# A block of two layers on one core: ends of stages, first pairs and first loads rearranged

## The chip, the core and the metric

One core of a Trainium2 chip. Five engines with their own instruction queues work on it: TensorE (PE in the profile; its weight loads are PEld), VectorE (DVE), ScalarE (ACT), GpSimd (POOL) and SyncE (SP), which here only issues transfers; POOL issues some too. Each queue runs in order; semaphores order the engines among each other. The metric is the device time of one execution in microseconds (us), lower is better; the kernel before has three such runs.

## What is computed

One block of a diffusion backbone for 256 latent and 256 context tokens of width 2048, float32, in two layers. Each layer is a mixer and a squared-ReLU MLP (2048 to 8192 and back), each between two norms and with a shift, a scale and a gate that a large matrix (`ada_w`) makes from the conditioning vector `c`.

```
layer 0:  h  = mod(norm(x));  xx = shifted(h) - h
          k, v, r  = (h + xx*mu) @ w_k, w_v, w_r          one mu each
          decay, a = low ranks of width 96 (two directions);  gate = low rank of width 256
          per head (32 of 64) and direction, token by token:
              S = S*decay - (S kk) b^T + v k^T;   out = S r       kk = norm(k*k_k), b = kk*a
          y  = (groupnorm(out) + bonus) * gate @ w_o
layer 1:  z = conv3(h @ in_w);  v, x1, x2 = split(z)
          y = x2 * conv(h2, x1 * conv(h1, v))       long filters h1, h2 from a small sine network
          y = y @ out_w
each:     x += gate * norm(y);   then the same around  relu(h @ up)^2 @ down
```

## The kernel before, in words

All large products run as three products of two halves: a float32 operand is cast to fp32r on ACT (`wh`, `xh`), the rest is subtracted on DVE (`wl`, `xl`), and PE adds hi*hi, hi*lo and lo*hi in one PSUM bank. `load_split` loads a block of weights on SP and splits it; `gemm_ws` keeps two column blocks of 128 in two banks (`mm`) over the whole contraction, `gemm_tok` one column block of 512 for two halves of the tokens (`tt`). With `lead` the first call takes two such groups at once in four banks. In the listing nearly all instructions of ACT, DVE and SP have line 53, the wrapper that records them, and those of PE line 111, so groups are told apart by their tiles.

The stages, in order: `start` loads and normalizes, makes the first shift and scale, mixes the tokens for the low ranks (`mix_split` 1, 4, 5) and for the key (`mix_split` 2, kept in `self.xs`), and multiplies the low ranks into six banks. `lora_hidden` empties these banks through `xt`. `rwkv_proj` is the key projection (`mm<-xh,wh`); in each half pair `tick` takes units of a background: second halves of the low ranks (`lora2`, 44 of its 80 units), the mixes of value and receptance (`mixes`, 24 units, tile `xs`, stored to memory as `xv`, `xr`), and `ada_w` columns on DVE (`acc`, 70 units). `rwkv_begin` runs the first two fills (`fill_r`, `fill_v`: products of value and receptance for a group of four heads, tile `fl`) beside the rest of the low ranks and the first group's preparation. `rwkv_scan` runs the recurrence in eight groups of eight steps in chunks of 64 tokens (tiles `VU`, `NT`, `KR`, `Z`), with the next group's fills and preparation between; in the last group `filters` takes the place of the fills: three sine layers, then sixteen blocks, each a product with split weights (`w4h`, `w4l`, tile `sg`) and a transform (`fl`). Then `rwkv_out`, the first MLP, `hyena`, the second MLP. Each of these four ends in `resid`: squares of the result's rows (`ysq`, `ss`), root, reciprocal, a diagonal matrix `dg`, and with it PE turns the result (`sg<-dg`), which is added to `x`.

The order of each queue comes from a planner: it simulates the program and picks for each engine the ready instruction that was traced first; `high_priority(n)` counts an instruction as traced n places earlier. Two things go ahead of it. `add_manual_dep` chains: while `self.pins` is a dict, every instruction of the engines in `self.pinned` is tied behind the one traced before it, so that these queues run in the order of the code. In `start` that is PE alone, in the loop of `rwkv_scan` (from `self.pins = {}` on) PE, ACT, DVE and SP. And a tile waits for the memory that an earlier pool used there: the scan's pools open when those of the projection close.

Of the kernel before, what the change touches and what calls it, by code (L numbers as in the profile page):

```python
# [18 lines left out]
P = 128  # L19
# [50 lines left out]
class Kern:  # L70
# [105 lines left out]
    def gemm_ws(self, W, K, ms, x, ntok, evac, lead=False):  # L176

        nk = K // P
        if lead:
            ps = [[self.mm.tile([P, 512], F32, name="mm") for _ in range(2)] for _ in range(2)]  # L180
            for k0 in range(0, nk, 4):
                w = [self.load_split(W[k0 * P : (k0 + 4) * P, m0 * P : (m0 + 2) * P].rearrange("(k p) n -> p k n", p=P), 4, 256)
                     for m0 in ms[:2]]
                for k in range(4):
                    for j in range(2):
                        for i in range(2):
                            self.mm3(ps[j][i][:, :ntok], self.cut(w[j][k], slice(i * P, (i + 1) * P)), x(k0 + k),
                                     k0 + k == 0, k0 + k == nk - 1)
                self.tick(self.rate)
            for j in range(2):  # L190
                for i in range(2):
                    evac(ms[j] + i, ps[j][i][:, :ntok])
            ms = ms[2:]
        for m0 in ms:
            ps = [self.mm.tile([P, 512], F32, name="mm") for _ in range(2)]
            for k0 in range(0, nk, 8):
                src = W[k0 * P : (k0 + 8) * P, m0 * P : (m0 + 2) * P].rearrange("(k p) n -> p k n", p=P)
                w = self.load_split(src, 8, 256)
                for k in range(8):
                    for i in range(2):  # L200
                        s = slice(i * P, (i + 1) * P)
                        self.mm3(ps[i][:, :ntok], self.cut(w[k], s), x(k0 + k),
                                 k0 + k == 0, k0 + k == nk - 1)
                self.tick(self.rate)
            for i in range(2):
                evac(m0 + i, ps[i][:, :ntok])

    def gemm_tok(self, W, x, evac, lead=False, stages=None):

        for ns in ((0, 1), (2,), (3,)) if lead else ((0,), (1,), (2,), (3,)):  # L210
            ps = {(n, tt): self.mm.tile([P, 512], F32, name="mm") for n in ns for tt in range(2)}
            for k0 in range(0, KT, 4):
                if stages and len(ns) > 1:
                    stages(k0)
                for n in ns:
                    w = self.load_split(W[k0 * P : (k0 + 4) * P, n * 512 : (n + 1) * 512].rearrange("(k p) n -> p k n", p=P), 4, 512)
                    for k in range(k0, k0 + 4):
                        for tt in range(2):
                            self.mm3(ps[n, tt], self.cut(x(k), slice(tt * P, (tt + 1) * P)), w[k - k0], k == 0, k == KT - 1)
# [122 lines left out]
    def ada_scan(self, n, pool):  # L342
# [4 lines left out]
        nc.vector.memset(wide, 0.0)  # L347
        nc.vector.tensor_copy(wide[:, :, 0], self.sc2[:, 0, :])
        pick = pool.tile([P, 2], F32, name="pick", bufs=1)
        nc.vector.memset(pick, 0.0)  # L350
        for j in range(4):
            nc.vector.tensor_tensor(pick, pick, self.ident[:, 32 * j : 32 * j + 2], op=ALU.add)
# [75 lines left out]
    def resid(self, x, y, ss, layer, gi, ch, pool, nxt=None):  # L428
# [12 lines left out]
        for n in range(1, 4):  # L441
            nc.vector.tensor_tensor(ss[:, 0, :], ss[:, 0, :], ss[:, n, :], op=ALU.add)
        nc.scalar.activation(ss[:, 1, :], ss[:, 0, :], AF.Sqrt, bias=self.eps[:, 0:1], scale=1.0 / D)
        nc.vector.reciprocal(ss[:, 1, :], ss[:, 1, :])
        dg = pool.tile([P, 2, P], F32, name="dg", bufs=1)
        for tt in range(2):
            nc.vector.tensor_scalar(dg[:, tt], self.ident, ss[:, 1, tt : tt + 1], None, op0=ALU.mult)
# [33 lines left out]
    def filters(self, es):  # L481
# [3 lines left out]
        p2 = self.pool(es, "f2", 2)  # L485
        fw = p1.tile([33, 64], F32, name="fw")
# [10 lines left out]
        for m, (lhs, n) in enumerate(((fw[:], 64), (w23[:], 64), (w3[:].rearrange("p a b -> p (a b)"), P))):  # L497
# [13 lines left out]
            if m == 2:  # L511
                self.tables()
            yield
# [9 lines left out]
        dft = []  # L523
        for i, nm in enumerate(("dftc", "dfts")):
            dft.append(self.dft_load(nm, p1, p2, "hf", 3))
        w4s = []

        def load(i):
            dc, o = divmod(i, 2)
            if dc < 4:  # L530
                w4 = p2.tile([P, 512], F32, name="w4")
                for b in range(2):
                    c0 = (b * 2 + o) * D + dc * 512
                    nc.sync.dma_start(w4[64 * b : 64 * b + 64, :], I["f_w4"][0, :, c0 : c0 + 512])
                w4s.append(w4)

        def skip(i):
            dc, o = divmod(i, 2)
            if dc < 4:
                self.sk = p2.tile([P, 512], F32, name="sk", bufs=1)[0:1, :]  # L540
                nc.sync.dma_start(self.sk, I["skip"][0, o : o + 1, dc * 512 : (dc + 1) * 512])

        def window(dc):
            if dc < 4:
                self.win = p2.tile([P, 2, 512], F32, name="win", bufs=1)
                nc.sync.dma_start(self.win, I["window"][:, dc * 512 : (dc + 1) * 512].rearrange("(a p) d -> p a d", p=P))

        window(0), load(0), skip(0)

        def first(dc, o, e, put):  # L550

            if not e:
                w4 = w4s.pop(0)
                self.w4 = split2(w4)
                load(2 * dc + o + 1)
            for tt in range(2):
# [4 lines left out]
                if o and e and tt:  # L561
                    window(dc + 1)
                if e == 0 and tt == 0:
# [6 lines left out]

        def split2(x):
            return self.split_into(p2.tile([P, 512], F32R, name="w4h")[:], x[:], p2.tile([P, 512], F32R, name="w4l")[:])
# [85 lines left out]
    def shifted(self, k):  # L658
# [3 lines left out]
        t = self.xt.tile([P, 512], F32, name="sx", bufs=2)  # L662
# [85 lines left out]
    def rwkv_proj(self, l2, ad1):  # L748
# [6 lines left out]
        self.bg, self.rate = [self.beside(mixed, self.NLOW + 24, ad, n)], (self.NLOW + 24 + n) / 15  # L755
# [17 lines left out]
        self.gemm_ws(I["w_k"][0], D, range(0, KT, 2), lambda k: xs[k], 512, evk)  # L773
# [179 lines left out]
    def rwkv_begin(self):  # L953
# [5 lines left out]
        for _ in self.beside(itertools.chain(self.fill_v(0), self.fill_r(1)), 48, self.low, n - n // 8 + .1):  # L959
            self.tick(self.BEG)  # L960
# [3 lines left out]
    def rwkv_scan(self, es, prep_pools, ngroups=KT // 2):  # L964
# [486 lines left out]
    def rwkv_out(self, xp):  # L1451
        nc, tc = self.nc, self.tc
        with tc.tile_pool(reuse_waits="tile", name="oy", bufs=16) as oy, tc.tile_pool(reuse_waits="tile", name="op", bufs=1) as op:
# [9 lines left out]

            def ev(n, tt, ps):
# [48 lines left out]
    PRT = 1  # L1513
# [4 lines left out]
    KEARLY = 16  # L1518
# [7 lines left out]
    SLACK = 0  # L1526
# [127 lines left out]
    def start(self, ap, xp):  # L1654
# [16 lines left out]
        self.pins, self.pinned = {}, ("pe",)  # L1671
# [5 lines left out]
        for q in range(4):  # L1677
# [4 lines left out]
            for k in range(4 * q, 4 * q + 4):  # L1682
# [5 lines left out]
                sx = self.shifted(k)  # L1688
                for n, m in enumerate((1, 4)):
# [8 lines left out]
        self.xs += [self.mix_split(2, k, True, self.xm) for k in range(self.KEARLY, KT)]  # L1698
# [171 lines left out]
```

## Time and profile before

| | us |
|---|---|
| three runs | 3592.66, 3605.2, 3619.01 (median 3605.2) |
| profiled execution | 3607.2 |
| its span in the trace | 3605.3 |
| `start` (to the key's first matmul) | 196.5 |
| key projection | 234.1 |
| `rwkv_begin` | 124.7 |
| scan, filters and last readout | 855.1 |
| `rwkv_out` to the first `dg` product | 101.3 |
| first MLP to its `dg` | 786.1 |
| `hyena` to its `dg` | 541.0 |
| second MLP to its `dg` | 750.5 |

The page tells the busy time of each engine; the stages above are cut from it at the first matmuls of each. PE means matmuls, PEld weight loads beside them. "Idle before" in a line is the time that the engine stood still before an instruction, with the work that ended it. PEclk is the clock that the chip granted PE, as a share of 2.4 GHz. SPq is SP's queue of transfers.

### The profile page before, as it was taken

What the parts mean: (1) busy time and instruction counts of PE and PEld (TensorE: products, weight loads), DVE (VectorE), ACT (ScalarE), POOL (GpSimd) and SP (SyncE); (2) the same over time, 40 slices, a digit from 0 to 9 for tenths busy, and PEclk for the clock granted to TensorE, in tenths of its full rate; (3) what the DMA queues carried; (4) which work ended last, traced back from release to release, by engine and by line L of the source; (5) the groups of instructions that cost most, each with busy time, mean ns of one, the idle gap of its engine ahead of it and who ended that gap; (6) DMA issues with size and microseconds to landing.
All of it is one profiled execution on the core that took longest, in us unless ns stands there. A gap on an engine that the chain in (4) does not pass through costs nothing.

```text
span 3605.3 us, 74531 instructions
## 1 busy us (share of the span) xinstructions
PE 3326.2 (92%) x30598; PEld 2904.8 (81%) x30598; DVE 2457.0 (68%) x3867; ACT 1739.7 (48%) x3069; POOL 435.0 (12%) x496
## 2 busy tenths in 40 slices
PE   6799978989989788999999999999999899999999
PEld 3477777878888666898978889899887798989897
DVE  4788675767767655687777776587787675555554
ACT  4454454544544444443434435566664663434343
POOL 0011121111111000000000002034441540000000
PEclk8999998999999989999999999999999999999999
DMA  9678798988988635688888887566665775555553
GB/s 305 229 232 266 252 329 252 282 267 262 288 269 267 194 124 184 198 269 280 257 286 259 283 268 233 164 221 219 222 209 182 244 249 191 183 187 187 187 185 120
DMA packets 587807, 836.79 MB, mean 232 GB/s; under 512 B 39551, under 2 KB 373280, under 8 KB 587464
## 3 DMA queue, kind: packets, MB, share of 16 engines
q1 hardware_dynamic: 556360, 718.76, 62.1%
q0 software_dynamic: 31104, 113.26, 10.0%
q8 instruction: 239, 3.92, 0.5%
q14 instruction: 104, 0.85, 0.1%
HBM read 777.31 MB, written 54.59 MB: 231 GB/s over the span
## 4 chain that ended last, share of the span: by engine, by line
PE 49%; DMA 21%; DVE 14%; ACT 6%; issue 6%; POOL 2%; SPq 1%; ACTq 0%; DVEq 0%; POOLq 0%
PE mm L111 34%; DMA aw<-in_ada_w 10%; PE fl L111 5%; PE sg L111 5%; PE sc L111 4%; DVE wl L53 3%; DMA w<-in_mlp_down 2%; DVE acc L53 2%; DMA w<-in_mlp_up 2%; POOL acc L325 2%; ACT wh L53 2%; DVE tmp L53 1%; ACT aw L53 1%; DVE d L53 1%; DMA a<-a 1%
## 5 line engine op out<-in xcount | busy, mean ns | idle before, releaser
L53 DVE TENSOR_TENSOR wl<-w,wh 128x1024 fp32r<-128x1024 f32 (+1 forms) x716 | 918.6, 1288 | 548.7 <-ACT wh L53 546.8
L53 ACT CAST wh<-w 128x1024 fp32r<-128x1024 f32 (+1 forms) x716 | 738.1, 1043 | 744.4 <-PE mm L111 436.2
L111 PE MATMUL mm<-hxh,wh 128*128 128x258 f32 x2816 | 803.5, 287 | 13.2 <-DVE nt L53 11.9
L111 PE MATMUL mm<-hxh,wl 128*128 128x258 f32 x2816 | 801.5, 285 | 6.8 <-DVE wl L53 6.7
L111 PE MATMUL mm<-hxl,wh 128*128 128x258 f32 x2816 | 799.4, 284 | 0.0
L111 PEld LDWEIGHTS mm<-hxh,wh 128*128 128x128 f32 x2816 | 534.2, 190 | 17.0 <-DVE nt L53 13.8
L111 PEld LDWEIGHTS mm<-hxh,wl 128*128 128x128 f32 x2816 | 534.1, 190 | 10.7 <-DVE wl L53 9.3
L111 PEld LDWEIGHTS mm<-hxl,wh 128*128 128x128 f32 x2816 | 536.3, 190 | 1.8
L325 POOL TENSOR_TENSOR acc<-acc,aw 128x512 f32<-128x512 f32 x180 | 274.9, 1528 | 1360.2 <-ACT aw L53 1254.1
L111 PE MATMUL mm<-wh,uh 128*128 128x512 f32 x1024 | 405.4, 396 | 1.0 <-DVE nt L53 1.0
L111 PE MATMUL mm<-wl,uh 128*128 128x512 f32 x1024 | 400.5, 391 | 4.2 <-DVE wl L53 4.1
L111 PE MATMUL mm<-wh,ul 128*128 128x512 f32 x1024 | 402.3, 393 | 0.0
L53 DVE SCALAR_TENSOR_TENSOR acc<-aw,sc,acc 128x512 f32<-128x512 f32 x300 | 225.3, 751 | 89.6 <-DMA aw<-in_ada_w 87.0
L111 PEld LDWEIGHTS mm<-wl,uh 128*128 128x128 f32 x1024 | 192.3, 188 | 51.1 <-DVE wl L53 8.3
L111 PEld LDWEIGHTS mm<-wh,ul 128*128 128x128 f32 x1024 | 192.1, 188 | 45.6
L111 PEld LDWEIGHTS mm<-wh,uh 128*128 128x128 f32 x1024 | 192.3, 188 | 42.5 <-DVE nt L53 1.4
L111 PE MATMUL fl<-fh,fx 128*128 128x256 f32 x1024 | 213.1, 296 | 9.9 <-DMA fx<-xv 8.4
L53 ACT ACTIVATE aw<-aw,sc 128x512 f32<-128x512 f32 x180 | 125.8, 719 | 138.1 <-DMA aw<-in_ada_w 137.6
L111 PEld LDWEIGHTS fl<-fh,fx 128*128 128x128 f32 x1024 | 168.2, 193 | 27.9 <-issue 14.0
L111 PE MATMUL fl<-flo,fx 128*128 128x256 f32 x512 | 146.0, 285 | 0.4 <-issue 0.4
L111 PE MATMUL sg<-ard,KB 64*64 64x64 f32 (+1 forms) x3584 | 131.1, 247 | 13.5 <-ACT yf L53 4.8
L111 PE MATMUL mm<-xl,wh 128*128 128x512 f32 (+1 forms) x320 | 131.7, 412 | 12.1 <-DVE xl L53 12.0
(352 smaller groups left out, 5871.8 us busy)
## 6 DMA issues: line engine op xcount, KB each, us to landing
aw<-in_ada_w SPq DMA_DIRECT2D x288, 512.0 KB, 5.7
w<-in_mlp_down SPq DMA_DIRECT2D x128, 1024.0 KB, 5.1
w<-in_mlp_up SPq DMA_DIRECT2D x120, 1024.0 KB, 6.0
fx<-xv POOLq DMA_DIRECT2D x128, 512.0 KB, 6.2
aw<-in_ada_w SPq DMA_DIRECT2D x192, 256.0 KB, 3.0
w<-in_hy_in_w SPq DMA_DIRECT2D x44, 1024.0 KB, 6.2
fx<-xr POOLq DMA_DIRECT2D x64, 512.0 KB, 5.6
w<-in_w_k SPq DMA_DIRECT2D x16, 1024.0 KB, 5.7
```

The lines of the kernel that those rows point to most:

```text
L53: return self.kern.pin(self.key, f(*a, **kw))
L111: return self.pin("pe", self.nc.tensor.matmul(out, lhsT=lhsT, rhs=rhs, **kw))
L325: nc.gpsimd.tensor_tensor(acc, acc, w[:, a], op=ALU.add)
```

## The change

- `gemm_ws` and `gemm_tok`: in the last block of the contraction, the matmuls of the first bank (or pair, or half of the tokens) all come before those of the second. `gemm_tok`'s last column block (`3 in ns`) is emptied with priority PRT, now 400; the norm of `resid` up to `dg` has it too. `rwkv_out` calls one root of a small tile (`st`) before its products.
- `gemm_ws(first=...)`: the key's first pair takes two banks of pool `sc` instead of `mm`, and does not tick the background; the rate goes from 1/15 to 1/13 of the units.
- `KEARLY` 12 instead of 16: the last four key mixes are traced behind the loop over the low ranks, with the shift tiles kept (`sx` in four buffers).
- `LOWS` = 1.25: the rest of the low ranks is dealt out earlier among the fills.
- The first two `scan_values` (loads of `VU`) are traced first in `rwkv_scan` with priority PRS = 1000; the `memset`s and additions for `wide` and `pick` in `ada_scan` have PRS too.
- `filters`: the first loads of window, weights and skip come first; the two transform matrices are loaded and split between the sine layers; the weights of a block are split at the end of the block before (`weights`), not at its own beginning.

```diff
-    def gemm_ws(self, W, K, ms, x, ntok, evac, lead=False):
+    def gemm_ws(self, W, K, ms, x, ntok, evac, lead=False, first=None):
...
-                for k in range(4):
-                    for j in range(2):
-                        for i in range(2):
-                            self.mm3(ps[j][i][:, :ntok], ...)
+                order = [(j, k) for k in range(4) for j in range(2)]
+                for j, k in sorted(order) if k0 == nk - 4 else order:
+                    for i in range(2):
+                        self.mm3(ps[j][i][:, :ntok], ...)
...
-            ps = [self.mm.tile([P, 512], F32, name="mm") for _ in range(2)]
+            ps = first or [self.mm.tile([P, 512], F32, name="mm") for _ in range(2)]
...
-                self.tick(self.rate)
+                if not first:
+                    self.tick(self.rate)
...
+            first = None
...
-                    for k in range(k0, k0 + 4):
-                        for tt in range(2):
-                            self.mm3(ps[n, tt], ...)
+                    pairs = [(k, tt) for k in range(k0, k0 + 4) for tt in range(2)]
+                    for k, tt in sorted(pairs, key=lambda p: p[1]) if k0 == KT - 4 else pairs:
+                        self.mm3(ps[n, tt], ...)
...
-            for n in ns:
-                for tt in range(2):
-                    evac(n, tt, ps[n, tt])
+            with self.tc.high_priority(self.PRT if 3 in ns else 0):
+                for n in ns:
+                    for tt in range(2):
+                        evac(n, tt, ps[n, tt])
...
+        with self.tc.high_priority(self.PRS):          # ada_scan: wide, pick
...
+        with self.tc.high_priority(self.PRT):          # resid: ss, root, reciprocal, dg
...
+        def weights(i):                                # filters
+            halves.append(split2(w4s.pop(0)))
+            load(i)
+        halves, dft = [], []
+        window(0), load(0), load(1), skip(0)
...
             if m == 2:
                 self.tables()
+            else:
+                nm = ("dftc", "dfts")[m]
+                dft.append(self.dft_load(nm, p1, p2, "hf", 3))
+            if m == 1:
+                weights(2)
             yield
...
-                w4 = w4s.pop(0)
-                self.w4 = split2(w4)
-                load(2 * dc + o + 1)
+                self.w4 = halves.pop(0)
...
+                if e and tt and w4s:
+                    weights(2 * dc + o + 3)
...
-        t = self.xt.tile([P, 512], F32, name="sx", bufs=2)
+        t = self.xt.tile([P, 512], F32, name="sx", bufs=4)
...
-        self.bg, self.rate = [self.beside(mixed, self.NLOW + 24, ad, n)], (self.NLOW + 24 + n) / 15
+        self.bg, self.rate = [self.beside(mixed, self.NLOW + 24, ad, n)], (self.NLOW + 24 + n) / 13
...
-        self.gemm_ws(I["w_k"][0], ..., 512, evk)
+        self.gemm_ws(I["w_k"][0], ..., 512, evk, first=[self.sc.tile([P, 512], F32, name="sc") for _ in range(2)])
...
-        for _ in self.beside(itertools.chain(self.fill_v(0), self.fill_r(1)), 48, self.low, n - n // 8 + .1):
+        for _ in self.beside(itertools.chain(self.fill_v(0), self.fill_r(1)), 48, self.low, self.LOWS * (n - n // 8)):
...
+        with self.tc.high_priority(self.PRS):
+            for i in range(2):
+                self.scan_values(0, i)
         for _ in self.scan_products(0, 0):
             pass
         self.load_to(3 + self.AHEAD)
         self.feed_open(ngroups)
-        for i in range(2):
-            self.scan_values(0, i)
...
+            nc.scalar.activation(op.tile([P, 2], F32, name="st"), self.eps, AF.Sqrt)
...
-    PRT = 1
+    PRT = 400
-    KEARLY = 16
+    KEARLY = 12
+    LOWS = 1.25
+    PRS = 1000
...
-        self.xs += [self.mix_split(2, k, True, self.xm) for k in range(self.KEARLY, KT)]
+        self.xs += [self.mix_split(2, k, True, self.xm, sxs[k]) for k in range(self.KEARLY, KT)]
```

## Rows read from the trace of the kernel before

**Rows 1.** The page, part 1: busy us, share of span, instructions.

```profile
PE 3326.2 (92%) x30598; PEld 2904.8 (81%) x30598; DVE 2457.0 (68%) x3867; ACT 1739.7 (48%) x3069; POOL 435.0 (12%) x496
```

**Rows 2.** Windows: length, busy us of PE/PEld/DVE/ACT/POOL (count), PEclk, DMA share, GB/s.

```profile
196.50:430.60 234.10, 225.50 (x960) 180.65 (x960) 183.49 (x285) 105.20 (x168) 35.84 (x49) 0.96 0.79 261
...
1276.30:1403.00 126.70, 114.27 (x1224) 85.68 (x1224) 67.83 (x120) 57.55 (x124) 0.00 (x0) 0.94 0.36 118
```

**Rows 3.** Windows behind three stops.

```profile
2838.69:2846.00 7.31, 7.16 (x34) 6.68 (x35) 4.06 (x9) 4.96 (x11) 2.98 (x3) 0.59 0.78 260
562.80:575.50 12.70, 8.25 (x108) 7.14 (x108) 5.71 (x15) 3.84 (x10) 0.50 (x1) 0.52 0.57 172
196.50:200.00 3.50, 3.50 (x9) 2.81 (x10) 3.50 (x5) 3.48 (x8) 0.00 (x0) 0.58 0.77 223
```

**Rows 4.** DVE groups, 157 to 196.5: count, busy us, mean ns, idle before.

```profile
L53 DVE TENSOR_TENSOR xl<-xt,xh 128x512 fp32r<-128x512 f32 (+1 forms) x20 | 11.9, 615 | 0.0
L53 DVE SCALAR_TENSOR_TENSOR xt<-sx,cols,hall 128x512 f32<-128x512 f32 (+1 forms) x17 | 11.3, 681 | 0.0
L53 DVE SCALAR_TENSOR_TENSOR acc<-aw,sc,acc 128x512 f32<-128x512 f32 x12 | 8.9, 744 | 0.6 <-DMA aw<-in_ada_w 0.6
```

**Rows 5.** Order of time, PE: start, length, [idle before, releaser].

```profile
193.17 0.28 PE L111 MATMUL sg<-xh,wl 128*128 128x256 f32 x1
196.50 0.79 PE L111 MATMUL mm<-xh,wh 128*128 128x512 f32 x1 [3.05 <-ACT xt L53]
```

**Rows 6.** Waits, ACT, 196.5 to 430.6: total us, times, longest.

```profile
ACT xs L53 <- DMA xv<-xs: 31.4, 13, 5.0
```

**Rows 7.** Order of time, SP's queue, 524 to 574.

```profile
525.11 1.03 SPq L53 DMA_DIRECT2D v<-fe  x2
...
551.30 0.32 SPq L53 DMA_DIRECT2D gate<-l2t  x1
...
556.47 0.41 SPq L53 DMA_DIRECT2D fr<-in_w_v  x1
556.93 9.27 SPq L53 DMA_DIRECT2D VU<-v  x12
566.31 1.07 SPq L53 DMA_DIRECT2D aw<-in_ada_w  x2
```

**Rows 8.** Order of time, PE, 546 to 592.

```profile
562.83 1.04 PE L111 MATMUL sc<-VU,NT 64*64 64x64 f32 x12 [7.49 <-DMA VU<-v]
...
570.76 1.08 PE L111 MATMUL mm<-aw,wide 128*32 128x256 f32 x8 [4.43 <-DVE pick L53]
```

**Rows 9.** Order of time, DVE, same stretch.

```profile
556.24 0.42 DVE L53 TENSOR_TENSOR NT<-sg,masks 128x256 f32<-128x256 f32 x1
```

**Rows 10.** Waits, PE, 1276.4 to 1403.

```profile
PE sg L111 <- ACT w4h L53: 14.4, 7, 6.0
PE sg L111 <- DVE w4l L53: 1.4, 6, 0.2
```

**Rows 11.** Order of time, PE, at the four ends of stages.

```profile
1511.65 1.65 PE L453 MATMUL sg<-dg,o 128*128 128x128 f32 x6 [5.33 <-DVE dg L53]
...
2297.72 1.28 PE L453 MATMUL sg<-dg,o 128*128 128x128 f32 x8 [3.56 <-DVE dg L53]
...
2838.69 2.81 PE L453 MATMUL sg<-dg,y 128*128 128x128 f32 x9 [9.99 <-DVE dg L53]
...
3589.16 2.07 PE L453 MATMUL sg<-dg,o 128*128 128x128 f32 x8 [2.70 <-DVE dg L53]
```

**Rows 12.** Order of time, ACT, at the first and third end.

```profile
1509.49 1.28 ACT L53 ACT_TABLE_LOAD   x1
1510.78 0.30 ACT L53 ACTIVATE ss<-ss,eps 128x2 f32<-128x2 f32 x1
...
2831.55 1.33 ACT L53 ACTIVATE aw<-aw,sc 128x512 f32<-128x512 f32 x2 [2.93 <-DMA aw<-in_ada_w]
```

**Rows 13.** Order of time, PE, first MLP's first stop.

```profile
1557.98 0.58 PE L111 MATMUL mm<-hxh,wh 128*128 128x258 f32 x1 [3.66 <-DVE nt L53]
```

More of the change, by code (lines that the diff above doesn't have):

```diff
@@ L346, in ada_scan @@
         wide = pool.tile([P, KT, 32], F32, name="wide", bufs=1)
-        nc.vector.memset(wide, 0.0)
-        nc.vector.tensor_copy(wide[:, :, 0], self.sc2[:, 0, :])
         pick = pool.tile([P, 2], F32, name="pick", bufs=1)
-        nc.vector.memset(pick, 0.0)
-        for j in range(4):
-            nc.vector.tensor_tensor(pick, pick, self.ident[:, 32 * j : 32 * j + 2], op=ALU.add)
+        with self.tc.high_priority(self.PRS):
+            nc.vector.memset(wide, 0.0)
+            nc.vector.tensor_copy(wide[:, :, 0], self.sc2[:, 0, :])
+            nc.vector.memset(pick, 0.0)
+            for j in range(4):
+                nc.vector.tensor_tensor(pick, pick, self.ident[:, 32 * j : 32 * j + 2], op=ALU.add)
         todo = [(layer, ch, i, half, k4) for layer, ch, i in itertools.islice(self.ada_todo, n) for half in range(2) for k4 in range(4)]
@@ L439, in resid @@
                 self.split_into(hi[:, :, c], self.mod[:, nxt[0], nxt[2], :], lo[:, :, c])
[L441 to L444, printed above, removed]
         dg = pool.tile([P, 2, P], F32, name="dg", bufs=1)
-        for tt in range(2):
-            nc.vector.tensor_scalar(dg[:, tt], self.ident, ss[:, 1, tt : tt + 1], None, op0=ALU.mult)
+        with self.tc.high_priority(self.PRT):
+            for n in range(1, 4):
+                nc.vector.tensor_tensor(ss[:, 0, :], ss[:, 0, :], ss[:, n, :], op=ALU.add)
+            nc.scalar.activation(ss[:, 1, :], ss[:, 0, :], AF.Sqrt, bias=self.eps[:, 0:1], scale=1.0 / D)
+            nc.vector.reciprocal(ss[:, 1, :], ss[:, 1, :])
+            for tt in range(2):
+                nc.vector.tensor_scalar(dg[:, tt], self.ident, ss[:, 1, tt : tt + 1], None, op0=ALU.mult)
         def add(k):
@@ L485, in filters, with load, skip, window @@
         p2 = self.pool(es, "f2", 2)
+        w4s = []
+        def load(i):
+            dc, o = divmod(i, 2)
+            if dc < 4:
+                w4 = p2.tile([P, 512], F32, name="w4")
+                for b in range(2):
+                    c0 = (b * 2 + o) * D + dc * 512
+                    nc.sync.dma_start(w4[64 * b : 64 * b + 64, :], I["f_w4"][0, :, c0 : c0 + 512])
+                w4s.append(w4)
+        def skip(i):
+            dc, o = divmod(i, 2)
+            if dc < 4:
+                self.sk = p2.tile([P, 512], F32, name="sk", bufs=1)[0:1, :]
+                nc.sync.dma_start(self.sk, I["skip"][0, o : o + 1, dc * 512 : (dc + 1) * 512])
+        def window(dc):
+            if dc < 4:
+                self.win = p2.tile([P, 2, 512], F32, name="win", bufs=1)
+                nc.sync.dma_start(self.win, I["window"][:, dc * 512 : (dc + 1) * 512].rearrange("(a p) d -> p a d", p=P))
+        def weights(i):
+            halves.append(split2(w4s.pop(0)))
+            load(i)
+        def split2(x):
+            return self.split_into(p2.tile([P, 512], F32R, name="w4h")[:], x[:], p2.tile([P, 512], F32R, name="w4l")[:])
+        halves, dft = [], []
+        window(0), load(0), load(1), skip(0)
         fw = p1.tile([33, 64], F32, name="fw")
@@ L522, in filters @@
         zz = [split(z, n, p1) for z, n in ((zs, "zs"), (zd, "zd"))]
[L523 to L548, printed above, removed]
         def first(dc, o, e, put):
             if not e:
-                w4 = w4s.pop(0)
-                self.w4 = split2(w4)
-                load(2 * dc + o + 1)
+                self.w4 = halves.pop(0)
             for tt in range(2):
@@ L569, in first @@
                 yield
-        def split2(x):
-            return self.split_into(p2.tile([P, 512], F32R, name="w4h")[:], x[:], p2.tile([P, 512], F32R, name="w4l")[:])
         def second(dc, o, e, hl):
@@ L771, in evk @@
                                  start=m == 0 and x is sh, stop=m == KT - 1 and x is sl)
-        self.gemm_ws(I["w_k"][0], D, range(0, KT, 2), lambda k: xs[k], 512, evk)
+        self.gemm_ws(I["w_k"][0], D, range(0, KT, 2), lambda k: xs[k], 512, evk, first=[self.sc.tile([P, 512], F32, name="sc") for _ in range(2)])
         ri = ev.tile([P, 512], F32, name="kt")[:NH]
```

10 lines of the change are left out of this document (5 added, 5 removed).

## The prediction, made before the changed kernel ran

> **What bounds the kernel now.** I read the page's busy times first: TensorE (PE) is busy 92% of the span and no other engine comes near [rows 1]. So a change pays where PE stands still, and by what PE stands still. Next come the busy times by stretch: PE is busy 225.5 us of 234.1 in the key projection and 114.3 of 126.7 in the filters' main stretch [rows 2]. Third, the lists of waits and the order of time at the ends of the stages, which tell what ended each stop. Last, the granted clock behind the stops: after three of them PE ran near 1.2 GHz instead of 2.4 for 3.5, 12.7 and 7.3 us (granted 0.58, 0.52, 0.59) [rows 3]. A stop that goes can give back part of that too.
>
> **The change, part by part.** Gains are PE time, against the profiled execution's own 3607.2 us.
>
> *Start to key projection.* The low ranks' last matmul starts at 193.17 us; the key's first waits 3.05 us until ACT has emptied a bank [rows 5]. Two banks of the sc pool are free there, so the wait can go: 3.05. The nine slow matmuls behind it (3.5 us at 0.58) would take some 1.5 us less. The four last key mixes go behind the low ranks' mixes. Each is one DVE multiply-add and one subtraction, 0.681 + 0.615 us on the mean, so 5.2 us leave a DVE that hardly rests there; but 12 operations of the next stage (8.9 us of acc) run in the same stretch and will fill part of the room [rows 4]. I take half, 2.6. The shift tiles in four buffers cost nothing: they hold the same results longer, and no instruction is added. **7.2 us**, between 0 (weight tiles come free only with the low ranks' last matmuls, so the split may be the next thing late) and 9.8.
>
> The first pair no longer ticks the background, so its 138 units (44 + 24 + 70) are spread over the 14 other half pairs, at 1/13 instead of 1/15 of them each. I cost that at nothing: DVE is busy 183.5 us of 234.1 and POOL 35.8 [rows 2]. Without that cover it is the second rival.
>
> *Begin and first scan group.* PE waits 7.5 us for the first values [rows 8]. They were stored at 525.1, but their loads went out at 556.93, behind the last gate store of the low ranks (551.30) and a weight load [rows 7]. LOWS = 1.25 ends the low ranks after 32/40 x 48 = 38 of 48 fill steps instead of at the end, and the eight early loads get priority. Then the mask product NT is late next: it starts at 556.24 and takes 0.42 [rows 9], while PE's work ended at 555.34 (562.83 less 7.49, rows 8): 1.4 us stay, 6.1 go. Of the 12.7 us at 0.52 with 8.25 busy, half clock cost 4.0; I take 1.5, since a stop follows. That stop, 4.4 us for DVE's pick [rows 8], I leave in place though its instructions get priority 1000: they are issued while all four queues of the scan are chained in written order, behind the group's preparation, and priority cannot pass a chain. This part of the change does nothing, I think (0 to 4.4). **7.6 us**, between 2 and 15.4.
>
> On SP the eight loads move past the weight loads of the fill. By the rows SP issued nothing else in the 9.27 us of the twelve value loads, and the next load left at 566.31 [rows 7]. If the early loads wait for a store to land, the fill's weights stand behind them; that is the first rival. The Trainium skill says so too (DMA: Bandwidth & Descriptors, Anatomy of one DMA): a DMA's wait for a semaphore is held by the issuing sequencer, not by the DMA engines.
>
> *Filters.* PE waits 14.4 us in 7 stops for w4h and 1.4 in 6 for w4l [rows 10]. The change splits the next weights at the end of the block before. The first stop (6.0) mostly stays, because the same casts and those of the two transform matrices now stand between the sines, on the same chain: 0.6 gained. Of the other 8.4 + 1.4 = 9.8 I take 8: the subtraction now stands in front of a block's last hfl. The stretch has 12.4 us of PE idle in all [rows 2], so it can give this. The six loads put in front of the first layer's weights delay a load that PE does not wait for. **8.6 us**, between 0 and 14.
>
> *Ends of stages.* PE waits for dg 5.33, 3.56, 9.99 and 2.70 us [rows 11]. At the last nothing competes, so 2.7 is the chain itself (copy, square, root, reciprocal, dg). Priority 400 lets the other three come down to it: 2.6 + 0.9 + 7.3. At the third, ACT stood 2.93 us for a modulation weight with the squares behind it [rows 12]; an in-order queue may keep that, so I take 5 of 7.3, and 2 of the 2.9 us that half clock cost behind it (7.16 busy at 0.59). Finishing one token half first brings its copy forward, which at the last border is already beside matmuls: 0. **10.5 us**, between 5 and 14.
>
> In the first of these the table load of 1.28 us leaves the border; the root starts 0.01 us after it [rows 12], so 1.28 is its whole price and it is inside the 2.6. The Trainium skill (ScalarE: Activation LUTs, What ACT_TABLE_LOAD costs) adds a drain of 1.38 us to each switch; by it the sum would be 1.4 us larger and a new dummy root between two other functions dearer, but no drain is seen in these rows.
>
> *Lead stages, reordered.* The stop behind the first (3.66 us) is for DVE's nt [rows 13], which needs the norm's root, not a bank: **0**, at most 3.7.
>
> Sum: 7.2 + 7.6 + 8.6 + 10.5 = 33.9, so 3573.3 for such an execution. It ran 2.0 us above the median of the runs (3605.2), so 3571 against the median; I say **3572**. All low ends: 7 gained, 3598. All high: 57, 3548.
>
> **The rivals.** *First: the stops move to the DMA.* SP holds the early value loads and the fill's weights behind them, ACT stands for the modulation weight, the first pair for its splits. Then the parts give about 2 + 2 + 8 + 5 = 17: 3588. For: the SP and ACT rows above. Against: eight of the 33.9 us lie in the filters, where nothing new is loaded late. Chance 0.22.
>
> *Second, slower: the key projection chokes on its background.* The mixes have one buffer, and ACT stands 31.4 us in 13 waits until a mix has left for memory [rows 6], with weight casts queued behind. Nearly all of it is hidden today behind the split tiles ahead. In 14 ticks instead of 16 the waits lie closer. If they came through whole, PE would lose 31 us, and at least 1.5 us of half clock (as after the 3.05 us stop) behind each of 13: 20 more, and the 7.2 of the first part. From half of the waits on it eats the rest of the gain; whole it is 51 + 7 - 34 = 24 slower, 3629. Against: PE is idle only 8.6 us in that stretch [rows 2]. Chance 0.09.
>
> *Third: the high ends.* The chain does not hold pick back, the freed DVE goes to the low ranks alone, the third border falls to 2.7: about 50, 3555. Chance 0.12.
>
> **How the numbers follow.** The forecast has 0.57 and its own range of 3556 to 3590. 1% is 36 us, about what a measurement of this kernel tells from no change: faster means under 3569. From the forecast 0.24 lies there, from the third rival 0.12, from the first 0.01: 0.37. Slower by over 1% is the second rival where it comes whole, 0.08; within 1% 0.55. The range 3550 to 3604 leaves out the second rival and the outer tails.
>
> **What would show it.** Right: the key's first matmul within 1 us of the low ranks' last and ahead of the copy out of their banks; VU's loads before 550 us and PE's wait for them under 2 us, with a wait for pick of about 4 us still there; no w4h waits in the filters except the first; dg waits near 2.7 us at the first two borders and under 6 at the third. Wrong: new stops in the fill for fr, ACT waits for xs that reach PE in the key projection, or the four ends shorter and the time of later stages longer by as much.

## The result

The changed kernel takes 3577.5 us (median of 8 runs, 3562.8 to 3583.9) against 3604.2 for the kernel before: 26.8 us by the medians; ratio 0.9929, 95% interval 0.9912 to 0.9946, or 25.6 us. A second series beside other kernels gave 0.9939 (0.9917 to 0.9961). The forecast was 3572. It held, but three of its four terms were too large, one of them altogether; the fourth, the filters, was about right.

The profiled execution (span 3561.0 us) is the fastest of the eight, some 15 us under their median, so its difference of 44 us to the profile before is not the change's worth. Read alone it would put 10 us into the scan, which varies by as much (below). The page, then PE at the places that the prediction names (start, length, idle before and its releaser; lines between are left out at "..."):

```profile
PE 3312.7 (93%) x30598; PEld 2890.3 (81%) x30598; DVE 2450.2 (69%) x3867; ACT 1738.5 (49%) x3070; POOL 435.3 (12%) x496
```

```profile
186.72 0.28 PE L111 MATMUL sg<-xh,wl 128*128 128x256 f32 x1
186.84 0.40 PE L111 MATMUL sc<-xh,wh 128*128 128x512 f32 x1
...
551.54 0.62 PE L111 MATMUL sc<-VU,NT 64*64 64x64 f32 x14 [1.16 <-DVE NT L53]
...
560.34 1.08 PE L111 MATMUL mm<-aw,wide 128*32 128x256 f32 x8 [6.89 <-DMA aw<-in_ada_w]
...
1255.77 0.79 PE L111 MATMUL sg<-w4h,zsh 128*128 128x512 f32 x1 [3.29 <-ACT zsh L53]
...
1472.27 2.07 PE L459 MATMUL sg<-dg,o 128*128 128x128 f32 x8 [4.25 <-DVE dg L53]
...
2253.21 2.08 PE L459 MATMUL sg<-dg,o 128*128 128x128 f32 x8 [3.36 <-DVE dg L53]
...
2792.44 2.07 PE L459 MATMUL sg<-dg,y 128*128 128x128 f32 x8 [9.56 <-DVE dg L53]
...
3546.06 1.34 PE L459 MATMUL sg<-dg,o 128*128 128x128 f32 x8 [2.63 <-DVE dg L53]
```

Against [rows 5]: the key's first product follows the low ranks' last without a stop. Against [rows 8]: the wait for the values (7.49) is now 1.16 for NT, the one for pick (4.43) is now 6.89 for a modulation weight. Against [rows 10]: no wait for w4h is left among the filters' waits of over 1 us. Against [rows 11]: the four waits for dg are hardly shorter; what stood in front of the third is the same as before. ACT of the changed kernel there, the modulation weight ahead of the square, as in [rows 12]:

```profile
2785.30 1.33 ACT L53 ACTIVATE aw<-aw,sc 128x512 f32<-128x512 f32 x2 [2.73 <-DMA aw<-in_ada_w]
2786.55 0.61 ACT L53 ACTIVATE ysq<-y 128x512 f32<-128x512 f32 x1
```

Windows of the changed kernel (length, busy us of PE, PEld, DVE, ACT and POOL, PEclk, DMA share, GB/s): at the three places of [rows 3], then its filters up to the first product of w_o:

```profile
186.84:190.34 3.50, 3.33 (x16) 2.43 (x15) 3.50 (x5) 2.49 (x4) 0.00 (x0) 1.00 0.00 0
560.34:573.04 12.70, 12.70 (x199) 10.94 (x199) 5.81 (x10) 6.17 (x17) 1.96 (x4) 0.87 0.72 206
2792.44:2799.75 7.31, 7.16 (x41) 6.73 (x42) 3.70 (x8) 4.41 (x10) 2.54 (x2) 0.76 0.80 261
...
1255.77:1375.35 119.58, 106.88 (x1224) 82.08 (x1224) 68.37 (x127) 59.76 (x130) 0.00 (x0) 0.97 0.43 140
```

The clock at the head of the key is at its full level (1.00, against 0.58 in [rows 3]).

### The profile page after: what moved, and what is told of

The parts are those of the page before. It is cut to its first block, busy times and chain, and to the rows that moved or that the text cites. A ratio compares the mean times of both kernels' runs of the same rounds, so it can differ in the third digit from the quotient of the medians.

```text
span 3561.0 us, 74541 instructions
## 1 busy us (share of the span) xinstructions
PE 3312.7 (93%) x30598; PEld 2890.3 (81%) x30598; DVE 2450.2 (69%) x3867; ACT 1738.5 (49%) x3070; POOL 435.3 (12%) x496
## 4 chain that ended last, share of the span: by engine, by line
PE 54%; DMA 19%; DVE 14%; ACT 6%; issue 5%; POOL 2%; SPq 0%; ACTq 0%; DVEq 0%; POOLq 0%
PE mm L111 39%; DMA aw<-in_ada_w 10%; PE fl L111 5%; PE sg L111 5%; PE sc L111 4%; DVE wl L53 3%; POOL acc L329 2%; DVE acc L53 1%; DVE tmp L53 1%; DVE d L53 1%; ACT aw L53 1%; ACT wh L53 1%; DMA w<-in_mlp_down 1%; DVE xt L53 1%; DMA cum<-cum 1%
## 5 line engine op out<-in xcount | busy, mean ns | idle before, releaser
L53 DVE SCALAR_TENSOR_TENSOR acc<-aw,sc,acc 128x512 f32<-128x512 f32 x300 | 225.0, 750 | 102.7 <-DMA aw<-in_ada_w 100.5
L111 PEld LDWEIGHTS mm<-wl,uh 128*128 128x128 f32 x1024 | 192.4, 188 | 48.6 <-DVE wl L53 5.7
L111 PEld LDWEIGHTS sg<-ard,KB 64*64 64x64 f32 x3584 | 110.0, 136 | 20.1 <-ACT yf L53 4.7
```

What stands on the lines that cost most here:

```text
L53: return self.kern.pin(self.key, f(*a, **kw))
L111: return self.pin("pe", self.nc.tensor.matmul(out, lhsT=lhsT, rhs=rhs, **kw))
```

## The experiments

Twelve runs follow: eleven edited kernels, and the changed one once more (after2). Since one profile can be 15 us off as a whole, each was profiled, and the stages are compared one by one: a stage that an edit does not touch is a repeat of the same code. All in us, from the traces. "Key first" and "key end" are the starts of the key's first and last matmul; "begin" is from the first fill to the scan's first modulation product, "filters" from the wait in the last group (sg<-ident,VU) to the first product of w_o; "w_o" is from there to the first dg product, "second MLP" from the third dg product to the fourth.

| kernel | ratio to before | key first | key end | begin | filters | w_o | third dg wait | second MLP |
|---|---|---|---|---|---|---|---|---|
| before | 1 | 196.5 | 430.3 | 131.4 | 180.8 | 101.3 | 9.99 | 750.5 |
| after | 0.9929 | 186.8 | 423.4 | 127.6 | 166.5 | 96.9 | 9.56 | 753.6 |
| after2 | 0.9939 | 185.6 | 418.4 | 130.7 | 167.2 | 100.5 | 9.46 | 750.7 |
| u_filters | 0.9986 | 190.9 | 426.9 | 130.4 | 174.6 | 100.9 | 8.31 | 754.8 |
| u_begin | 0.9954 | 189.1 | 424.8 | 131.6 | 166.3 | 99.8 | 9.74 | 751.6 |
| u_key | 0.9954 | 197.4 | 428.4 | 128.4 | 168.9 | 96.9 | 9.87 | 750.4 |
| u_ends | 0.9932 | 187.6 | 423.4 | 126.3 | 167.8 | 100.0 | 7.07 | 753.2 |
| p_filters | 0.9979 | 196.6 | 426.8 | 133.5 | 165.5 | 99.2 | 6.91 | 753.1 |
| u_kearly | one run | 191.1 | 424.8 | 128.8 | 166.3 | 96.4 | 9.90 | 753.9 |
| x_ada | 0.9918 | 185.7 | 419.0 | 122.5 | 168.8 | 96.6 | 9.86 | 751.3 |
| x_gate | 0.9950 | 186.7 | 421.2 | 127.8 | 169.9 | 98.3 | 4.03 | 756.8 |
| x_split | 0.9948 | 186.9 | 420.1 | 129.8 | 166.8 | 94.6 | 7.05 | 755.0 |
| x_best | 0.9944 | 189.2 | 430.8 | 122.9 | 168.3 | 98.1 | 7.46 | 754.8 |
| x_all | 0.9933 | 187.1 | 424.4 | 122.4 | 167.6 | 96.3 | 2.64 | 762.6 |

The intervals of the ratios are 0.0014 to 0.003 (5 to 11 us) to each side: times separate the filters, hardly anything else.

**One part undone.** The filters:

```diff
 def filters(...):      # whole function up to `second`: as before
-    window(0), load(0), load(1), skip(0)   # first
-    ... dft_load and weights(2) between the sines; weights(...) at the end of a block
+    ... dft_load behind the sines; window(0), load(0), skip(0); split2 at the head of a block
```

> The changed kernel with the filters of the kernel before (weights split at the head of their block, transforms loaded and split behind the sines, loads in the old order). Theory from the two traces: the part is worth 14.5 us, 7.1 us of PE idle and 7.4 us of PE busy time that half clock cost (granted 0.93 against 0.97); so this kernel runs 14 to 15 us above the changed one, near 3592, ratio to before near 0.997, and its stretch from the first filter product to the first of w_o is 134 us again. By the sum of the prediction it was 8.6: near 3586, stretch 128. Rival: the stretch gets shorter only because its loads are issued earlier beside a quieter scan, then the stretch is under 125 us here too.

Ratio 0.9986 (0.9968 to 1.0004): the largest part. The stretch from the first filter product to w_o is 130.0 us, against 119.2 to 122.6 in all twelve profiles with the new filters. The rival is wrong. Between the two sizes this does not decide: 130.0 lies nearer to the 128 of the sum than to the 134 of the theory.

The beginning of the scan:

```diff
-        ... self.LOWS * (n - n // 8)):
+        ... n - n // 8 + .1):
-        with self.tc.high_priority(self.PRS):
-            for i in range(2): self.scan_values(0, i)
         ...
         self.feed_open(ngroups)
+        for i in range(2): self.scan_values(0, i)
-    PRS = 1000
+    PRS = 0
```

> The changed kernel with the old beginning of the scan: low ranks dealt out to the end of the fills, first values loaded behind the first products, no priority for wide and pick. Theory: PE waits 7.5 us for the values again and 4.4 for pick, the wait of 6.9 us for the modulation weight goes, so the first modulation product comes 4 us later than in the changed kernel; the 5 us that the next 90 us of the scan gained go too if they follow from it (19.5 + 95.4 us again for the two stretches behind), and stay (19.2 + 90.3) if they are variation between runs. Total 4 to 9 us above the changed kernel: 3581 to 3587. By the sum 7.6: 3585. Rival: the changed beginning only exchanges waits, and the total is the changed kernel's, 3577.

Ratio 0.9954 (0.9939 to 0.9968). The old waits are back, PE in order of time:

```profile
557.94 1.06 PE L111 MATMUL sc<-VU,NT 64*64 64x64 f32 x12 [7.34 <-DMA VU<-v]
565.90 1.08 PE L111 MATMUL mm<-aw,wide 128*32 128x256 f32 x8 [4.42 <-DVE pick L53]
```

"Begin" is 132.2 us on the mean of the three kernels with the old beginning and 128.7 of the eight with the new one alone: 3.4 us, not 7.6. The scan behind it, from that modulation product to the wait in the last group, is as short with the old beginning (650.2 us) as in the first profile of the changed kernel (648.5, against 658.8 before), so that part of the 44 us did not follow from it.

The key:

```diff
-        ..., evk, first=[self.sc.tile(...) for _ in range(2)])
+        ..., evk)
-    self.rate = (self.NLOW + 24 + n) / 13
+    self.rate = (self.NLOW + 24 + n) / 15
-    KEARLY = 12
+    KEARLY = 16
-    name="sx", bufs=4
+    name="sx", bufs=2
```

> The changed kernel with the old beginning of the key projection: first pair in the banks of the low ranks, all key mixes ahead, background over 16 half pairs. Theory: the key projection ends 6.9 us later (430.7 against 423.8) and nothing behind it changes: 3584, ratio 0.995. Rival: the lower number of half pairs for the background costs something later, then the difference is below 4 us.

Ratio 0.9954 (0.9934 to 0.9973). Key's first product comes at 197.4 behind the same stop of 3.05 us, and its end at 428.4 is 5.0 later than in the first profile of the changed kernel: as expected in kind, less in size.

The ends of stages:

```diff
-    PRT = 400
+    PRT = 0
-    for j, k in sorted(order) if k0 == nk - 4 else order:
+    for j, k in order:                      # gemm_tok's pairs likewise
-            nc.scalar.activation(op.tile([P, 2], ...), self.eps, AF.Sqrt)
```

> The changed kernel without what was done at the ends of stages: no priority for the norm and the emptying, no joined order of the last blocks, no early root. By the sum of the prediction it loses 10.5 us (3588). By the traces the four waits for dg only fell from 5.33, 3.56, 9.99, 2.70 to 4.25, 3.36, 9.56, 2.63, 1.8 us together, and a new wait of 2.2 us for x came behind the first: then this part is worth 0 to 2 us and the time is 3577 to 3580, ratio 0.993; the first MLP's 7 us are then variation or come from the joined orders, and its length here (740 or 733 us) tells which.

Ratio 0.9932 (0.9913 to 0.9952): no difference can be measured. First wait 5.38 us, third 7.07. The first MLP, counted from its stop for nt to the second dg product, was 738.5 us here, 732.6 and 743.2 in the two profiles of the changed kernel and 739.7 before: variation.

**What varies.** The changed kernel once more, unedited:

> The changed kernel once more, beside those below. It separates what varies between executions from what the change does: its first profile stood 14.7 us under the median of its runs, and the scan between the first groups and the last took 631 us in it, against 641 before. If that was the change, the scan is within 631 to 636 here too; if it varied, it may be anywhere from 631 to 648. Ratio to before 0.993 again; if all single parts are worth what leaving them out cost (0.0057, 0.0025, 0.0025 and 0.0003 of the time), 0.989.

0.9939. Left out one by one, the four parts had cost 0.011 of the time together; the 0.989 that would follow lies outside the interval here (0.9917 to 0.9961), so single runs overstate the parts. The scan, counted as above, took 652.1 us here, 644.8 to 656.8 in the profiles with the new filters and 662.9 in u_filters (the expectation's 631 and 641 are of a stretch some 18 us shorter). The list of waits of PE between 600 and 1200 us (total, times, longest) holds most of the difference between u_filters and the changed kernel's first profile, on one line, of the changed kernel and then of u_filters; DVE, ACT and SP run the same instructions in the same order there in both:

```profile
PE mm L111 <- DMA aw<-in_ada_w: 1.0, 3, 0.5
```

```profile
PE mm L111 <- DMA aw<-in_ada_w: 11.1, 6, 4.2
```

The two kernels with the old filters have the two longest scans (658.8 and 662.9). Whether the filters have a part in that is open: the profile of u_filters is 16 us above the median of its own runs.

**Does the order written by hand hold pick?**

```diff
         nxt = load(0)                       # in ada_scan
         tail = iter(())
+        yield
...
         with self.tc.high_priority(self.PRS):
             for i in range(2): self.scan_values(0, i)
+            next(ada)                       # a block of its own; ahead of self.pins = {}
```

> The changed kernel with the scan's first modulation unit opened ahead of the hand-chained order: wide and pick are made, and the first weight tile is loaded, before the first values. Theory: the written order alone kept pick (ready 559.0) and the weight load (issued 552.96, behind three fill weights) late, so the wait of 6.9 us for the weight, in which the wait for pick had hidden, goes: the first modulation product comes within 2 us of the last product ahead of it, total 5 to 7 us under the changed kernel, and the half clock behind it may give back 1 more. Rival: the DMA engines are full there (share 1.04), the values then come later by as much, and the sum of the two waits stays near 8 us.

0.9918 (0.9895 to 0.9941); "begin" 122.5, and 122.9 and 122.4 in the two later kernels that contain the edit: on the mean 6.1 us under the eight with the new beginning but without the edit. SP and DVE of the changed kernel, then SP and PE of this one:

```profile
540.15 8.97 SPq L53 DMA_DIRECT2D VU<-v  x12
550.82 0.38 SPq L53 DMA_DIRECT2D r<-fe  x1
551.30 1.56 SPq L53 DMA_DIRECT2D fr<-in_w_v  x3
552.96 1.28 SPq L53 DMA_DIRECT2D aw<-in_ada_w  x2
```

```profile
556.83 0.69 DVE L53 TENSOR_TENSOR KB<-KB,ei 128x512 f32<-128x512 f32 x1
557.58 0.48 DVE L53 MEMSET wide<- 128x512 f32 x1
558.09 0.18 DVE L53 COPY wide<-sc 128x16 f32<-128x16 f32 x1
558.22 0.06 DVE L53 MEMSET pick<- 128x2 f32 x1
558.34 0.75 DVE L53 TENSOR_TENSOR pick<-pick,ident 128x2 f32<-128x2 f32 x4
```

```profile
538.72 1.31 SPq L53 DMA_DIRECT2D VU<-v  x1
540.13 0.53 SPq L53 DMA_DIRECT2D aw<-in_ada_w  x1
540.70 7.45 SPq L53 DMA_DIRECT2D VU<-v  x11
```

```profile
550.47 0.64 PE L111 MATMUL mm<-aw,wide 128*32 128x256 f32 x8
```

In the changed kernel pick still stands behind the group's preparation (KB) and is done at 559.1; the weight, issued behind the values and three weights of the fill and landing while the DMA engines are full (share 1.05 from 553.0 to 560.3), arrives 1.2 us after that, at 560.3, and so its name stands at the wait. Traced ahead of the chain, both are there in time, and the values are no later (1.16 us for NT again). Theory right.

**What holds the third end, and the first MLP's lead?**

```diff
+    # ada_run, second MLP: each ACT scaling behind resid's root of the third end;
+    #          first MLP: the first DVE sum of a column behind the norm's reciprocal
+    with self.tc.issue_after(gate): nc.scalar.activation(w[:, a] ..., AF.Identity, scale=s)
+    with self.tc.issue_after(gate): nc.vector.tensor_scalar(acc, w[:, a], s, ...)
```

> The changed kernel with the modulation work of the two MLPs held back: in the second, ACT takes its scaled columns only behind the root of the third end; in the first, DVE starts its sums only behind the reciprocal of the norm. Theory: the third wait for dg is 7 to 10 us because ACT stands for a modulation weight with the squares behind it (2.73 us and two scalings, 2.7); it falls to 5 or less. In the first MLP's lead the wait of 2.2 us for x goes and the wait for nt falls from 4.1 to about 2. Together 6 to 9 us under the changed kernel. Rival: the weights' splits of the next stage keep both engines as long, and the waits stay within 1 us.

0.9950 (0.9929 to 0.9970): not faster. The third wait fell to 4.03 and no wait of 1 us was left in the first MLP's lead, but nothing of it can be measured at the end: the first MLP took 783.7 us from dg to dg (780.9 and 791.7 in the changed kernel), and `hyena` and the second MLP together 1290.4 (1290.0 to 1299.2 in the ten profiles of kernels that hold nothing back). PE's waits of the first MLP, of the changed kernel (lead, then the rest) and of this one (the rest):

```profile
PE mm L111 <- DVE nt L53: 4.1, 1, 4.1
PE sg L459 <- DVE x L53: 2.8, 2, 2.2
...
PE mm L111 <- DVE nt L53: 5.9, 5, 1.5
PE mm L111 <- DVE wl L53: 2.3, 6, 0.9
```

```profile
PE mm L111 <- DVE wl L53: 8.9, 9, 2.2
PE mm L111 <- DVE nt L53: 6.2, 6, 1.5
```

6.9 us left the lead, and the waits for wl and nt behind it grew from 8.2 to 15.1, most of it for wl (2.3 to 8.9). That fits sums which still have to be made, now in front of the weight splits; the order on DVE was not traced for it.

**Is it the weight splits that priority cannot pass?**

```diff
+    # load_split, first two blocks of each MLP (self.root, self.dgi: resid's root and last dg)
+    with self.tc.issue_after(self.root): nc.scalar.copy(h, v)
+    with self.tc.issue_after(self.dgi): nc.vector.tensor_tensor(l, v, h, op=ALU.subtract)
```

> The changed kernel with the first two weight splits of each MLP held back: the casts behind the root, the subtractions behind dg. Theory: at the first end a cast that waits for its load, and the subtraction behind it, stand ahead of the copies and squares in every version, and priority changed nothing there; without them the copy of the first half runs beside the last products, and the first wait for dg falls from 4.25 to 2.7 to 3.0; at the third end one cast and one subtraction leave (2.7 us of work) and the wait falls by 1 to 2.5. Rival: the splits are then late for the first products of the MLP (two casts of 1.05 and two subtractions of 1.22 us), and a new wait for wh or wl of 2 us or more stands behind the dg products.

First wait 2.64, third 7.05: both as expected, and no new wait for wh or wl of 2 us. (The third proves nothing: u_ends and p_filters have 7.07 and 6.91 without the edit.) DVE at the first end, of the changed kernel and of this one:

```profile
1467.06 1.23 DVE L53 TENSOR_TENSOR wl<-w,wh 128x1024 fp32r<-128x1024 f32 x1 [2.13 <-ACT wh L53]
1468.20 1.28 DVE L53 COPY o<-mm 128x512 f32<-128x512 f32 x2
1469.82 1.23 DVE L53 TENSOR_TENSOR wl<-w,wh 128x1024 fp32r<-128x1024 f32 x1 [0.34 <-ACT wh L53]
1471.20 0.16 DVE L53 TENSOR_TENSOR ss<-ss 128x2 f32<-128x2 f32 x1 [0.15 <-ACT ysq L53]
```

```profile
1464.65 0.69 DVE L53 COPY o<-mm 128x512 f32<-128x512 f32 x1 [4.71 <-PE mm L111]
1465.78 0.69 DVE L53 COPY o<-mm 128x512 f32<-128x512 f32 x1 [0.44 <-PE mm L111]
1467.32 0.16 DVE L53 TENSOR_TENSOR ss<-ss 128x2 f32<-128x2 f32 x1 [0.85 <-ACT ysq L53]
```

In the changed kernel the two copies wait together behind a subtraction, whose cast waited for its load (ACT: 1.73 and 2.30 us for w<-in_mlp_up). With the splits held back the joined order does what it was written for: the first copy runs beside the last products. Yet the ratio, 0.9948 (0.9925 to 0.9972), shows no gain.

**Filters alone**, on the kernel before (the three other parts undone as above):

> The kernel before with the changed filters alone. If the parts simply add, this one runs 10 to 13 us under the kernel before (from the end of the last group's preparation to the first product of w_o 168 us, against 181 and 175 with the old filters), ratio 0.9965. Rival: with the beginning as it was, the filters' gain is partly taken by what else is late there, 5 us or less; or what leaving the part out cost (0.0053 of the time, 19 us) is its whole worth, then 0.9947.

0.9979 (0.9958 to 1.0001): 7.6 us, 0 to 15; the stretch is 165.5. The parts may add; the interval is too wide for more.

**Mixes or banks?** The one edit is `KEARLY = 16`.

> The changed kernel with all sixteen key mixes ahead of the low ranks' end again, but the first pair still in the free banks. Of the 7.2 us of the key's beginning the prediction gave 4.6 to the banks and 2.6 to the mixes. If so, the key projection ends 2.6 us later than in the profiles of the changed beginning (mean 422.2, 418.4 to 426.9), near 425, PE waits again 1 to 2.5 us several times for xl between 175 and 190, and no wait of 3.05 us stands at its head. Rival: without the late mixes the free banks do nothing, because the four mixes decide when the last low ranks run, and it ends at 429 as in the kernel before.

There is no stop at the key's head, which is at 191.1; the key ends at 424.8, as expected. So against 196.8 (mean of the old) and 187.6 (of ten with both), the banks bring 5.7 us at the head and the mixes 3.5, by this one profile; the ten range from 185.6 to 190.9. PE's waits for xl between 150 and 200 were 5.1 us in 6 here, 10.8 before and 3.5 in the changed kernel.

**Together:**

> The changed kernel with the first modulation unit ahead of the hand-chained order, and with the first two splits of each MLP held back. If both gains stay: 7 us from the scan's beginning and 1.5 + 2.4 from the first and third wait for dg, 0.991 of the kernel before and 10 us under the changed kernel. Rival: what the ends give is given back in the MLP behind, then it is the time of the first of the two alone, 0.992.

> The same with the modulation work of the MLPs held back too. The third wait for dg falls to 3 to 4 us (from 9.5) and the waits in the first MLP's lead go; if that stays, 6 to 10 us under the one before it, 0.989. In the kernel that held it back alone the first MLP was no shorter for it (783.7 us between its two ends against 779 to 792) and the second 3 us longer: by that, the work stands in front of weight splits later, and the time is within 3 us of the one before it.

0.9944 (0.9914 to 0.9973) and 0.9933 (0.9910 to 0.9956): neither is measurably faster than the changed kernel, and the 0.991 and 0.989 hoped for lie outside the intervals, the first barely. In x_all the third wait is 2.64, the chain's own length, and the second MLP behind it 762.6 us, 8 to 12 longer than in the kernels that hold no modulation work back. One piece of the return is in sight, 76 us behind that end:

```profile
2792.56 0.38 PE L470 MATMUL sg<-dg,y 128*128 128x128 f32 x1 [2.64 <-DVE dg L53]
...
2868.95 0.37 PE L319 MATMUL sg<-ones,acc 128*128 128x2 f32 x1 [3.53 <-POOL acc L338]
```

x_ada is the one version whose gain stands in the traces of three kernels; that its total beats the changed kernel's (0.9918 against 0.9929 and 0.9939) lies within the intervals.

## Why the prediction held, step by step

**Key: 7.2 forecast, 5.3 measured** (end 428.5 on the mean of three old, 423.2 of ten new). At the head it was worth 9.2 (196.8 to 187.6), near the upper bound of 9.8. But the projection itself became 4.0 longer (231.7 to 235.7): "I cost that at nothing" was the failing step. Of the 4.0, 3.3 are PE's idle time (9.3 to 12.6 on the same means). The second rival's mechanism does not show, however. ACT's waits until a mix has left for memory are of two kinds; [rows 6] has one (31.4 in 13). The other before, then both in the changed kernel between 186.8 and 423.8 us:

```profile
ACT xs L53 <- DMA xr<-xs: 23.0, 6, 6.8
```

```profile
ACT xs L53 <- DMA xv<-xs: 49.2, 16, 6.0
ACT xs L53 <- DMA xr<-xs: 14.1, 6, 4.4
```

Together they grow from 54.4 to 63.3 us, and u_key and p_filters, with the old key, have 59.7 and 62.3. PE waits 0.2 us for a weight split. It waits for the background's own products, the second halves of the low ranks; before, then changed:

```profile
PE sc L111 <- ACT l2h L53: 2.2, 1, 2.2
PE sc L111 <- DVE l2l L53: 0.3, 1, 0.3
```

```profile
PE sc L111 <- DVE l2l L53: 3.1, 4, 1.9
PE sc L111 <- ACT l2h L53: 3.0, 2, 1.8
PE sc L111 <- ACT l2t L53: 2.3, 2, 1.3
```

On the means of three old and ten new these waits are 3.5 and 5.7. Whether the 14 half pairs, the four late mixes or the two banks taken from sc cause it was not separated (u_kearly: 233.7, one profile).

**Begin: 7.6 forecast, 3.4 measured.** The values came as forecast (1.16 for NT, 1.4 expected), and pick stayed behind the chain as forecast. What failed is "I leave that stop in place": the stop behind does not keep its length when the one ahead shrinks. It ended by the clock of DVE and SP, not by PE's arrival; the first rival's queue (values, then weights on SP) put the modulation weight last. The prediction held the Trainium skill's rule (DMA: Bandwidth & Descriptors, Anatomy of one DMA) against SP, that a sequencer holds a DMA's wait. SP's rows show no wait of a value load here, so this case does not test the rule; the twelve issues take 8.97 us by themselves. x_ada shows that another 6.1 us were there to be had.

**Filters: 8.6 forecast, 10.2 measured** (177.7 on the mean of two old, 167.5 of twelve new; the two old ones are 6 us apart). The mechanism is right, and so is its size: the waits for w4h and w4l behind the first stop (9.8 us before, 10.4 in u_filters) are gone, at most 0.2 is left, and PE's idle time from the first filter product to w_o falls from 20.0 to 12.6 on the means, 7.4 where 8 was forecast. The first stop fell by more than the 0.6 assumed (6.04 and 6.03 to between 3.3 and 4.2), but nothing came of it: from the wait in the last group to the first filter product it is 46.7 and 44.7 us in the old ones and 45.5 to 48.5 in the new. What remains is PE's busy time, with as many matmuls. The same windows of before and of u_filters, the two with the old filters:

```profile
1276.26:1410.37 134.11, 114.31 (x1225) 85.73 (x1225) 69.42 (x127) 58.60 (x127) 0.00 (x0) 0.93 0.39 125
1273.96:1403.93 129.97, 109.75 (x1224) 81.89 (x1225) 69.13 (x127) 59.96 (x129) 0.00 (x0) 0.97 0.40 129
```

The twelve new ones are busy 106.7 to 109.9 us at 0.93 to 0.97. So the 7.4 us of busy time between the first two profiles (114.3 and 106.9) go with the granted clock, but that the change brought them is not shown: u_filters has the same stops as before, and the clock of the changed kernel.

**Ends: 10.5 forecast, about 0 measured** (by the times of u_ends, to within some 9 us). This is the term that failed. "Priority 400 lets the other three come down to it" is wrong: the copies stood behind the next stage's splits and ACT's squares behind its scalings in the changed kernel as before. x_split and x_gate take these away one by one (2.64 at the first end; 4.03 at the third), and x_all reaches 2.64 at the third. The planner's simulated loads came earlier than the real ones, I think: a cast that is ready in the plan is placed ahead of a copy that is not yet ready, whatever its priority. That reading of the plan itself was not tested; that these instructions stand ahead and cost the time was. The first wait fell from 5.33 to 4.25 because the table load left it (now at 1368.43, in the wait for w_o's first tile). u_ends, with the load back, has 5.38: 1.1 us, close to its 1.28, and no drain beside it, where the Trainium skill (ScalarE: Activation LUTs, What ACT_TABLE_LOAD costs) adds a drain of 1.38 to each switch. The third wait differs by 3 us for the same code (9.99 in before, 6.91 in p_filters), so that it is 1.5 longer on the mean with priority (9.5 in seven kernels, 8.0 in three) is not shown to mean anything.

**Lead, 0 forecast:** the wait for nt is 4.07 after 3.66 in the first MLP, with one of 2.18 for x ahead of it. The one for x is not the ends' doing: u_ends and p_filters have 1.9 and 2.0.

The stretch of w_o up to the first dg product is 1.9 us shorter (100.2 on the mean of the three kernels without this part, 98.3 of eight with it), of which that load is 1.1. From there to the end of the stop for nt it is 2.2 longer (46.5 on the mean of the same three, 45.3 to 47.8; 48.6 of the seven that hold nothing back, 47.4 to 51.6), so little stays: the prediction's own sign of being wrong, shorter ends and later stages longer by as much.

Measured sum: 5.3 + 3.4 + 10.2 + 0 = 18.9, against 25.6 by the first series' ratio (19.5 to 31.7) and 22 by the second's (14 to 30). The forecast's 33.9 lies above all of these. The 3 to 7 us between 18.9 and the ratios stand in no stage that was compared, so the account by parts is not closed. Its range held the time because it took in the first rival, which came true at two of its places, the queue of SP and ACT's modulation weight; at all of them it gave 3588. That 3577.5 came so near to 3572 is in part luck: the 10.5 of the ends were missing, and a few us that no term names were there.

## What to carry to other kernels

When a stop goes, work out when the next one ends by its own engines' and queues' clock; it will be as much longer as PE comes sooner. Do not count on an instruction's priority in a planned in-order queue to take it past work of the next stage; here 400 did not. Take that work away, or tie it behind, and then look where it comes back: in neither MLP did holding it back leave a gain that can be measured. Split a change by the stages of several profiles, not by one pair: untouched stages tell how far a difference can be trusted.

## What was not expected of the hardware

The same code ends the key projection anywhere from 418.4 to 430.8 us in ten profiles, and waits 1.0 us in one and 11.1 us in another for the same weight loads in the scan. A pair of profiles differed by 44 us where the medians differ by 27. And the same stop does not always bring the clock down: in the old filters PE ran near half clock behind one of 2.21 us (granted 0.54 from 1318.5 to 1326.0, before), and at full clock behind the same stop of 2.37 us in u_filters (1.00 from 1316.5 to 1324.0).
